# S5 mixer of the first layer: powers for the coefficient products read from a PSUM bank, their sums on GpSimd, phase squarings and one phase table on VectorE

## The chip, the cores and the metric

The kernel runs on one core of one Trainium2 chip. It is one program for a whole four-layer network on a sequence of 512 tokens. The metric is the device time of one execution in microseconds (us). Three runs of the kernel before took 1901.83, 1901.47 and 1900.82 us, median 1901.47.

## The reference, cut to what matters

The network has two blocks of two layers each, width 1024, all in float32. Only the mixer of the very first layer is touched, a state-space model (S5) with 64 groups of 16 channels and 64 complex states for each group:

```
u = (rms_norm(x) @ w_in)  as 64 groups x 16 channels
a = exp(lam * step)                        # one complex decay per group and state
b = cmul(f(a, lam), b)                     # input matrix 64 x 16 per group
x_t = a * x_(t-1) + b @ u_t                # complex recurrence over 512 tokens
y = Re(c @ x) + d * u
z = gelu(y);  out = val * sigmoid(gate),   val, gate = split(z @ w_glu)
```

The kernel works in chunks of eight tokens. For that it needs, for each group, the products of b and of c with the powers a^0 to a^8, complex, and for the recurrence over the 64 chunks it turns the complex state by a phase that grows with the chunk, then scans real numbers. The phases stand in "phase tables" (cosine and sine of 64 chunks for each group), which are made by doubling: from the phase powers e, e^2, e^4, ... each step computes the upper half of a table from its lower half.

## The kernel before, in words

The program is one list of instructions for the whole network. A class `Plan` records every operation that the code issues and works out who depends on whom from the regions of memory. One call of `emit` at the end puts all of them in a fixed order on each engine, by modelled costs and due times. So an edit in one place can move instructions elsewhere on all engines. One helper line issues all of them: L262 before, L263 after. For a PSUM bank the region is the whole bank.

In front of everything stands `layer0_mix`, which works on eight blocks m of eight groups (128 channels) each:

- `s5_params` computes the decay and the phase of each group from the inputs, on tiles of 128 partitions x 32 columns (the 8 x 64 states of a block are four columns of 128, and there are eight blocks). It squares the phase eight times to get the phase powers (tile `es`), with a normalisation after the third. One `square` is five GpSimd operations.
- `s5_table` makes one of four phase tables, for 8 of the 32 columns, in five doubling steps from width 2 to 64. Each step is two products and two sums. All four tables are made on GpSimd, tables 0 and 1 before the loop over the blocks and tables 2 and 3 within it.
- `s5_p` and `s5_q` make the coefficient matrices P = b x powers and Q = c x powers of a block. Both call `s5_cprod`: four products of 128x512 elements on VectorE, each with both operands spread by repeated reading, and two sums. The four products go to a ring of four buffers (tag `s5t`). The sums of P are on VectorE for blocks 0 and 1 and on GpSimd for blocks 2 to 7; all sums of Q are on VectorE.
- TensorE projects u block by block (`project`, 24 matmuls with split operands each), transposes P and multiplies for the kernels of a chunk (`s5_k`, `s5_pt`). `s5_u` multiplies a projection from its bank by the norm row `sbc` (a copy of a bank that all projections share). `s5_x` reads the states' input from a bank, multiplies it by cosine and sine on VectorE (the first rotation, two operations of 128x512), adds on GpSimd, scans and turns back.

Projections hold banks 0, 1, 2, 3, 5 and 6 before, in turn; 4 and 7 serve the small products. A bank of a projection comes free when `s5_u` has read it.

In the rows below, `s` is any tile of `layer0_mix`, `bank` a PSUM bank.

Of the kernel before, what the change touches and what calls it, by code (L numbers as in the profile page):

```python
# [24 lines left out]
KC = D // P  # L25
# [50 lines left out]
class Plan:  # L76
# [65 lines left out]
    @staticmethod  # L142
    def region(ap):

        if isinstance(ap, View):
            return ap.region()
        t, pat = ap.tensor, ap.ap
        if ap.space == bass.MemoryType.DRAM:
            return t.name, 0, 1, 0, 1
        if ap.space == bass.MemoryType.PSUM:  # L150
# [375 lines left out]
class Net:  # L526
# [306 lines left out]
    def s5_params(self, pool, prm):  # L833
# [13 lines left out]
        sq, c2 = mk_("sq"), mk_("c2")  # L847

        def square(yr, yi, xr, xi):
            G.tensor_tensor(sq, xi, xi, ALU.mult)  # L850
            G.tensor_tensor(c2, xr, xr, ALU.mult)
            G.tensor_tensor(yi, xr, xi, ALU.mult)
            G.tensor_tensor(yi, yi, yi, ALU.add)
            G.tensor_tensor(yr, c2, sq, ALU.subtract)
# [71 lines left out]
    def s5_table(self, pool, q, E):  # L926
# [6 lines left out]
        for i in range(1, 6):  # L933
# [21 lines left out]
    def s5_cprod(self, pool, out, x, tb, op0, op1, swap, E):


        V = self.nc.vector

        def prod(r, q):  # L960
            t = pool.tile([P, 4, 8, 16], F32, name=self.n("t"), tag="s5t", bufs=4)
            V.tensor_tensor(t, x[:, :, r].unsqueeze(2).to_broadcast([P, 4, 8, 16]),
                            tb[:, :, q].unsqueeze(3).to_broadcast([P, 4, 8, 16]), ALU.mult)
            return t.rearrange("p w j k -> p w (j k)")

        a, b = prod(0, 0), prod(1, 1)
        yield
        E.tensor_tensor(out[:, :, 0], a, b, op0)
        yield
        a, b = prod(1, 0), prod(0, 1)  # L970
        yield
        if swap:
            a, b = b, a
        E.tensor_tensor(out[:, :, 1], a, b, op1)

    def s5_q(self, pool, m, ld):

        q = pool.tile([P, 4, 2, P], F32, name=self.n("Q"), tag="s5Q", bufs=3)
        return q, self.s5_cprod(pool, q, ld[1], self.af[:, 4 * m : 4 * m + 4], ALU.add, ALU.subtract, True, self.nc.vector)

    def s5_p(self, pool, m, ld):

        pp = pool.tile([P, 4, 2, P], F32, name=self.n("P"), tag="s5P", bufs=1)
        return pp, self.s5_cprod(pool, pp, ld[0], self.pw[:, 4 * m : 4 * m + 4, :, 8:0:-1], ALU.subtract, ALU.add, False,
                                 self.nc.vector if m < 2 else self.nc.gpsimd)

    def s5_k(self, pool, m, bh, q):

# [116 lines left out]
    def layer0_mix(self, pool):  # L1105
# [9 lines left out]
            self.stat_add("n", self.x[m], m)  # L1115

        zs = []
        self.banks(g=(0, 1, 2, 3, 5, 6), r=(4, 7), s=(7,), o=(4,))
# [37 lines left out]
        sbc = self.bcast(pool, self.rms_col("n", D), 1)  # L1156
        next(params)
        next(params, None)
        self.drain(self.s5_table(pool, i, G) for i in range(2))
# [46 lines left out]
        def whole(start, gens, m):  # L1206
            start(m)
            while m in gens:
                go(gens, m)

        for m in range(6):
            project(m)
# [14 lines left out]
        for i in range(KC + 2):  # L1227
# [26 lines left out]
            go(qg, m)  # L1254
            go(qg, m)
            go(qg, m)
            if i == 0:
                project(7, lambda: w7)
                self.banks(g=(0, 1, 2, 3), r=(4, 5, 7), y=(6,))
            if 0 <= i - 2 < KC:  # L1260
                glu_part(i - 2)
            if 0 <= i - 1 < KC:
                zt[i - 1] = self.s5_o(pool, yt.pop(i - 1))
            if m < KC:
                prep_pe(m)
        self.banks(g=(4, 5, 6, 7), s=(4, 5), t=(6,), o=(7,))
        for m in range(2):
            glu(m, parts[2 * m], parts[2 * m + 1])
# [958 lines left out]
```

## Time and profile before

| | kernel before |
|---|---|
| runs | 1901.83, 1901.47, 1900.82 us; median 1901.47 |
| profiled execution | 1901.8 us, of which span of the instructions 1899.8 us |
| mean granted TensorE clock | 0.98 |
| TensorE busy | 1835.4 us, 97% of the span |
| VectorE busy | 1169.3 us, 62% |
| ScalarE busy | 837.1 us, 44% |
| GpSimd busy | 578.1 us, 30% |
| DMA | 157.85 MB, mean 83 GB/s |

The shares are means over the whole program. The touched work lies in the first 270 us, most of it between 30 and 155 us, so that the stretches there have to be read by themselves. In a window's row an engine is followed by its busy time and its number of instructions. [...]

### The profile page before, as it was taken

The numbers are of one execution on the slowest core, as the hardware profiler recorded it, in microseconds if no ns is written. First come the engines' busy times: TensorE is split into PE (matmuls) and PEld (weight loads), VectorE is DVE, ScalarE is ACT, GpSimd is POOL, SyncE is SP. The second block draws the span as 40 slices with busy tenths as digits, with TensorE's granted clock in tenths as the row PEclk, the third lists the DMA queues.
The fourth block names the chain that finished last, engine by engine and source line by source line (L and its number), as shares of the span: only waits on it lengthen the run. The fifth ranks groups of instructions, "written<-read, shape, count | busy, mean of one in ns | idle before, by whom it ended". The sixth has DMA issues, their size and how long they took to land.

```text
span 1899.8 us, 26981 instructions
## 1 busy us (share of the span) xinstructions
PE 1835.4 (97%) x10272; PEld 1474.4 (78%) x10272; DVE 1169.3 (62%) x2196; ACT 837.1 (44%) x1562; POOL 578.1 (30%) x707
## 2 busy tenths in 40 slices
PE   8789999999999999999999999999999999989997
PEld 5456788888888777778888888988778788768877
DVE  9898455444354778755534434563888763488875
ACT  4123342223233477744222222344767643566764
POOL 8984111001012166611100101540542071154205
PEclk9879999999999999999999999999999999999999
DMA  5322333323323221022232333332122132212113
GB/s 174 89 62 77 100 98 91 98 90 94 104 89 89 91 68 38 24 72 89 89 100 89 91 98 97 112 103 88 34 67 68 57 100 89 78 34 68 57 56 111
DMA packets 73136, 157.85 MB, mean 83 GB/s; under 512 B 26416, under 2 KB 34864, under 8 KB 73008
## 3 DMA queue, kind: packets, MB, share of 16 engines
q1 hardware_dynamic: 73008, 156.15, 27.0%
q8 instruction: 80, 1.31, 0.3%
q14 instruction: 48, 0.39, 0.1%
HBM read 150.81 MB, written 4.72 MB: 82 GB/s over the span
## 4 chain that ended last, share of the span: by engine, by line
PE 77%; DVE 8%; POOL 8%; ACT 4%; issue 2%; DMA 1%; SPq 0%; ACTq 0%; DVEq 0%; POOLq 0%
PE bank L262 77%; POOL s L262 3%; DVE bl L262 3%; DVE s L262 2%; POOL x L262 2%; POOL bl L262 1%; ACT bl L262 1%; DVE wl_r L262 1%; POOL acc_r L262 1%; ACT wh_r L262 1%; DVE xl_r L262 1%; DVE x L262 1%; ACT xh_r L262 0%; ACT bh L262 0%; DVE sm_r L262 0%
## 5 line engine op out<-in xcount | busy, mean ns | idle before, releaser
L262 ACT ACTIVATE wh_r<-wr_r 128x1024 fp32r<-128x1024 f32 (+2 forms) x270 | 278.1, 1031 | 587.0 <-PE bank L262 531.7
L262 PE MATMUL bank<-xh_r,wl_r 128*128 128x512 f32 (+1 forms) x1312 | 504.2, 388 | 4.5 <-DVE wl_r L262 4.4
L262 PE MATMUL bank<-xl_r,wh_r 128*128 128x512 f32 (+1 forms) x1312 | 504.6, 388 | 0.6 <-DVE xl_r L262 0.4
L262 PE MATMUL bank<-xh_r,wh_r 128*128 128x512 f32 (+1 forms) x1312 | 503.1, 389 | 1.1 <-ACT wh_r L262 1.1
L262 DVE TENSOR_TENSOR wl_r<-wr_r,wh_r 128x1024 fp32r<-128x1024 f32 (+2 forms) x270 | 372.3, 1380 | 159.2 <-ACT wh_r L262 153.1
L262 PEld LDWEIGHTS bank<-xh_r,wl_r 128*128 128x128 f32 x1312 | 249.0, 190 | 58.7 <-DVE wl_r L262 6.2
L262 PEld LDWEIGHTS bank<-xh_r,wh_r 128*128 128x128 f32 x1312 | 248.1, 190 | 55.6 <-issue 3.0
L262 PEld LDWEIGHTS bank<-xl_r,wh_r 128*128 128x128 f32 x1312 | 248.8, 190 | 52.5 <-issue 3.1
L262 POOL TENSOR_TENSOR ff<-ff,ff 128x512 f32<-128x512 f32 x44 | 62.6, 1422 | 590.2 <-DVE ff L262 575.0
L262 PE MATMUL bank<-ff,wh_r 128*128 128x512 f32 (+1 forms) x816 | 224.7, 363 | 0.3 <-ACT ff L262 0.2
L262 DVE TENSOR_TENSOR ff<-bank,ff 128x512 f32<-128x512 f32 x88 | 60.8, 691 | 223.5 <-PE bank L262 223.4
L262 PE MATMUL bank<-bh,wh_r 128*128 128x512 f32 (+1 forms) x656 | 179.3, 356 | 1.3 <-ACT bh L262 0.9
L262 PEld LDWEIGHTS bank<-ff,wh_r 128*128 128x128 f32 x816 | 145.3, 188 | 27.6 <-DVE ff L262 1.1
L262 PE MATMUL bank<-ff,wl_r 128*128 128x512 f32 (+1 forms) x408 | 146.6, 364 | 1.0 <-DVE wl_r L262 1.0
L262 DVE TENSOR_TENSOR x<-x,bank 128x256 f32<-128x256 f32 (+1 forms) x112 | 57.5, 529 | 130.9 <-PE bank L262 130.8
L262 PEld LDWEIGHTS bank<-bh,wh_r 128*128 128x128 f32 x656 | 113.9, 192 | 18.0 <-issue 2.4
L262 POOL TENSOR_TENSOR acc_r<-acc_r,sq_r 128x256 f32<-128x256 f32 (+1 forms) x63 | 75.0, 1191 | 160.8 <-ACT sq_r L262 160.7
L262 POOL TENSOR_TENSOR s<-s,s 128x32 f32<-128x32 f32 (+6 forms) x138 | 113.4, 846 | 30.4 <-DVE s L262 27.2
L262 PE MATMUL bank<-bh,wl_r 128*128 128x512 f32 (+1 forms) x328 | 113.6, 356 | 0.0
L262 DVE TENSOR_TENSOR s<-s,s 128x512 f32<-128x512 f32 (+4 forms) x124 | 93.9, 803 | 8.6 <-POOL s L262 8.3
L262 ACT ACTIVATE ff<-ff 128x512 f32<-128x512 f32 x88 | 55.0, 626 | 74.4 <-POOL ff L262 68.9
L262 PEld LDWEIGHTS bank<-ff,wl_r 128*128 128x128 f32 x408 | 76.3, 188 | 13.5 <-DVE wl_r L262 1.2
(257 smaller groups left out, 2834.2 us busy)
## 6 DMA issues: line engine op xcount, KB each, us to landing
wr_r<-w_gu SPq DMA_DIRECT2D x88, 512.0 KB, 3.5
wr_r<-w_in2f SPq DMA_DIRECT2D x48, 512.0 KB, 3.2
wr_r<-w_dn SPq DMA_DIRECT2D x37, 448.0 KB, 3.4
wr_r<-w_out SPq DMA_DIRECT2D x22, 512.0 KB, 3.3
wr_r<-w_dn SPq DMA_DIRECT2D x16, 512.0 KB, 3.5
wr_r<-w_in2v SPq DMA_DIRECT2D x16, 512.0 KB, 3.8
wr_r<-w_glu SPq DMA_DIRECT2D x12, 512.0 KB, 3.6
wr_r<-w_o SPq DMA_DIRECT2D x8, 512.0 KB, 3.2
```

The lines of the kernel that those rows point to most:

```text
L262: lambda: f(*[real(v) for v in a], **{x: real(v) for x, v in k.items()}), load, rows, idle))
```

## The change

- The eight squarings and the normalisation run on VectorE. A `square` has four operations in place of five (46 GpSimd operations of 128x32 become 38 on VectorE).
- Phase table 0 is made on VectorE; tables 1, 2 and 3 stay on GpSimd.
- A new function `s5_powers` has ScalarE copy the powers for the coefficient products into bank 7: two copies for blocks 0 to 3 at once, then two for each of blocks 4 to 7 when the place of an earlier block comes free (ten copies). `s5_cprod` reads the powers there, as its first operand.
- Both sums of P are on GpSimd for all blocks, and the second of the two sums of Q. With that 12 of the 20 sums that VectorE made are GpSimd's.
- Projections have five banks (0, 1, 2, 3, 5) in place of six, small products 4 and 6; bank 7 belongs to the powers until the end of the loop. For this bank the planner tells regions apart (`parted`).

```
 class Plan:
...
+    parted = None
...
-        if ap.space == bass.MemoryType.PSUM:
+        if ap.space == bass.MemoryType.PSUM and t.name != Plan.parted:
             return t.name, 0, P, 0, 2048
...
         sq, c2 = mk_("sq"), mk_("c2")
 
         def square(yr, yi, xr, xi):
-            G.tensor_tensor(sq, xi, xi, ALU.mult)
-            G.tensor_tensor(c2, xr, xr, ALU.mult)
-            G.tensor_tensor(yi, xr, xi, ALU.mult)
-            G.tensor_tensor(yi, yi, yi, ALU.add)
-            G.tensor_tensor(yr, c2, sq, ALU.subtract)
+            V.tensor_tensor(sq, xi, xi, ALU.mult)
+            V.tensor_tensor(c2, xr, xr, ALU.mult)
+            V.scalar_tensor_tensor(yi, xr, 2.0, xi, ALU.mult, ALU.mult)
+            V.tensor_tensor(yr, c2, sq, ALU.subtract)
 
         cr, ci = mk_("cr"), mk_("ci")
         square(cr, ci, cs, sn)
         dr, di = mk_("dr"), mk_("di")
         square(dr, di, cr, ci)
         square(cr, ci, dr, di)
-        G.tensor_tensor(sq, ci, ci, ALU.mult)
-        G.tensor_tensor(c2, cr, cr, ALU.mult)
-        G.tensor_tensor(sq, sq, c2, ALU.add)
-        G.tensor_scalar(sq, sq, -0.5, 1.5, ALU.mult, ALU.add)
+        V.tensor_tensor(sq, ci, ci, ALU.mult)
+        V.tensor_tensor(c2, cr, cr, ALU.mult)
+        V.tensor_tensor(sq, sq, c2, ALU.add)
+        V.tensor_scalar(sq, sq, -0.5, 1.5, ALU.mult, ALU.add)
 
         es = self.es = pool.tile([P, 6, w, 2], F32, name="es")
-        G.tensor_tensor(es[:, 0, :, 0], cr, sq, ALU.mult)
-        G.tensor_tensor(es[:, 0, :, 1], ci, sq, ALU.mult)
+        V.tensor_tensor(es[:, 0, :, 0], cr, sq, ALU.mult)
+        V.tensor_tensor(es[:, 0, :, 1], ci, sq, ALU.mult)
         for i in range(1, 6):
             square(es[:, i, :, 0], es[:, i, :, 1], es[:, i - 1, :, 0], es[:, i - 1, :, 1])
         yield
...
             E.tensor_tensor(tab[:, :, 1, n : 2 * n], k1[:, :, 1], k2[:, :, 0], ALU.add)
             yield
 
+    def s5_powers(self, m0, m1):
+
+        g, to = slice(4 * m0, 4 * m1), slice(m0 % 4 * 4, (m1 - 1) % 4 * 4 + 4)
+        SC = self.nc.scalar
+        SC.activation(self.powers[:, 0, to], self.pw[:, g, :, 8:0:-1], AF.Copy)
+        SC.activation(self.powers[:, 1, to], self.af[:, g], AF.Copy)
+
     def s5_load(self, pool, m):
         g4 = slice(4 * m, 4 * m + 4)
         ld = lambda nm, w: pool.tile([P, 4, 2, w], F32, name=self.n(nm), tag="s5" + nm, bufs=2)
...
 
         def prod(r, q):
             t = pool.tile([P, 4, 8, 16], F32, name=self.n("t"), tag="s5t", bufs=4)
-            V.tensor_tensor(t, x[:, :, r].unsqueeze(2).to_broadcast([P, 4, 8, 16]),
-                            tb[:, :, q].unsqueeze(3).to_broadcast([P, 4, 8, 16]), ALU.mult)
+            V.tensor_tensor(t, tb[:, :, q].unsqueeze(3).to_broadcast([P, 4, 8, 16]),
+                            x[:, :, r].unsqueeze(2).to_broadcast([P, 4, 8, 16]), ALU.mult)
             return t.rearrange("p w j k -> p w (j k)")
 
         a, b = prod(0, 0), prod(1, 1)
         yield
-        E.tensor_tensor(out[:, :, 0], a, b, op0)
+        E[0].tensor_tensor(out[:, :, 0], a, b, op0)
         yield
         a, b = prod(1, 0), prod(0, 1)
         yield
         if swap:
             a, b = b, a
-        E.tensor_tensor(out[:, :, 1], a, b, op1)
+        E[1].tensor_tensor(out[:, :, 1], a, b, op1)
 
     def s5_q(self, pool, m, ld):
 
         q = pool.tile([P, 4, 2, P], F32, name=self.n("Q"), tag="s5Q", bufs=3)
-        return q, self.s5_cprod(pool, q, ld[1], self.af[:, 4 * m : 4 * m + 4], ALU.add, ALU.subtract, True, self.nc.vector)
+        return q, self.s5_cprod(pool, q, ld[1], self.powers[:, 1, m % 4 * 4 : m % 4 * 4 + 4], ALU.add, ALU.subtract, True,
+                                (self.nc.vector, self.nc.gpsimd))
 
     def s5_p(self, pool, m, ld):
 
         pp = pool.tile([P, 4, 2, P], F32, name=self.n("P"), tag="s5P", bufs=1)
-        return pp, self.s5_cprod(pool, pp, ld[0], self.pw[:, 4 * m : 4 * m + 4, :, 8:0:-1], ALU.subtract, ALU.add, False,
-                                 self.nc.vector if m < 2 else self.nc.gpsimd)
+        return pp, self.s5_cprod(pool, pp, ld[0], self.powers[:, 0, m % 4 * 4 : m % 4 * 4 + 4], ALU.subtract, ALU.add, False,
+                                 (self.nc.gpsimd, self.nc.gpsimd))
 
     def s5_k(self, pool, m, bh, q):
...
             self.stat_add("n", self.x[m], m)
 
         zs = []
-        self.banks(g=(0, 1, 2, 3, 5, 6), r=(4, 7), s=(7,), o=(4,))
+        self.banks(g=(0, 1, 2, 3, 5), r=(4, 6), s=(6,), o=(4,))
+        self.powers = self.bank[7].rearrange("p (a w r j) -> p a w r j", a=2, w=16, r=2)
+        Plan.parted = self.powers.tensor.name
         self.warm(pool.tile([P, 2, S], F32, tag="s5PT", bufs=2)[:, 0])
         prm = pool.tile([P, 3, 32], F32, name="prm")
         nc.urgent = True
...
         sbc = self.bcast(pool, self.rms_col("n", D), 1)
         next(params)
         next(params, None)
-        self.drain(self.s5_table(pool, i, G) for i in range(2))
+        self.s5_powers(0, 4)
+        self.drain(self.s5_table(pool, i, (V, G)[i]) for i in range(2))
         us, scr, ld, pp, pg, q, qg, ks, kt, pt, zt, xg_, yt, wa = ({} for _ in range(14))
 
         def project(m, w=None):
...
             start(m)
             while m in gens:
                 go(gens, m)
+            if gens is qg:
+                self.s5_powers(m + 4, m + 5)
 
         for m in range(6):
             project(m)
...
             go(qg, m)
             go(qg, m)
             go(qg, m)
+            if m + 4 < KC:
+                self.s5_powers(m + 4, m + 5)
             if i == 0:
                 project(7, lambda: w7)
-                self.banks(g=(0, 1, 2, 3), r=(4, 5, 7), y=(6,))
+                self.banks(g=(0, 1, 2, 3), r=(4, 5), y=(6,))
             if 0 <= i - 2 < KC:
                 glu_part(i - 2)
             if 0 <= i - 1 < KC:
                 zt[i - 1] = self.s5_o(pool, yt.pop(i - 1))
             if m < KC:
                 prep_pe(m)
+        Plan.parted = None
         self.banks(g=(4, 5, 6, 7), s=(4, 5), t=(6,), o=(7,))
         for m in range(2):
             glu(m, parts[2 * m], parts[2 * m + 1])
```

GpSimd, in the place of the first sums of P that it makes. Tile s5_25 is phase table 1, s5_56 and s5_57 the temporaries of a table's step, s5_42 the phase powers, s5_64 the matrix P, s5_45, s5_46, s5_53 and s5_54 the ring of products, s5_28 a matrix Q. Before:

```order
L262 TENSOR_TENSOR s5_56_296<-s5_25_265,s5_42_282 128x256
L262 TENSOR_TENSOR s5_57_297<-s5_25_265,s5_42_282 128x256
L262 TENSOR_TENSOR s5_25_265<-s5_56_296,s5_57_297 128x8x16 x2
L262 TENSOR_TENSOR s5_56_296<-s5_25_265,s5_42_282 128x512
L262 TENSOR_TENSOR s5_57_297<-s5_25_265,s5_42_282 128x512
L262 TENSOR_TENSOR s5_64_304<-s5_45_285,s5_46_286 128x4x128
L262 TENSOR_TENSOR s5_25_265<-s5_56_296,s5_57_297 128x8x32
L262 TENSOR_TENSOR s5_64_304<-s5_53_293,s5_54_294 128x4x128
```

After (s5_26 and s5_27 are tables 2 and 3, the row of sm4 belongs to the norm):

```order
L263 TENSOR_TENSOR sm4_r1_75_115<-sm4_r0_73_114,mhalf_81 128x4
L263 COPY s5_25_265<-s5_42_282 128x16
L263 COPY s5_26_266<-s5_42_282 128x16
L263 COPY s5_27_267<-s5_42_282 128x16
L263 TENSOR_TENSOR s5_64_304<-s5_45_285,s5_46_286 128x4x128
L263 TENSOR_TENSOR s5_64_304<-s5_53_293,s5_54_294 128x4x128
L263 TENSOR_TENSOR s5_56_296<-s5_25_265,s5_42_282 128x32
L263 TENSOR_TENSOR s5_28_268<-s5_54_294,s5_53_293 128x4x128
L263 TENSOR_TENSOR s5_57_297<-s5_25_265,s5_42_282 128x32
```

Before, the sums of block 2's P stand behind the large steps of table 1; now the sums of block 0 stand ahead of table 1's first step.

VectorE, around the copy of the norm row (s5_35, `sbc`). s5_44 and s5_58 are the powers of P and a block's b, s5_47 to s5_50 temporaries of the parameters, wl_r the low part of a weight. Before, the copy is the engine's instruction 100:

```order
L262 TENSOR_TENSOR s5_46_286<-s5_58_298,s5_44_284 128x512
L262 TENSOR_TENSOR s5_48_288<-s5_48_288,s5_49_289 128x32
L262 TENSOR_TENSOR s5_49_289<-s5_15_255,s5_1_241 128x32
L262 TENSOR_TENSOR s5_64_304<-s5_45_285,s5_46_286 128x4x128
L262 TENSOR_TENSOR s5_50_290<-s5_48_288,s5_47_287 128x32
L262 TENSOR_TENSOR s5_48_288<-s5_44_284,s5_1_241 128x32
L262 COPY s5_35_275<-bank7_76 128x512
L262 TENSOR_TENSOR wl_r2_141_125<-wr_r0_5_87,wh_r2_139_124 128x1024
```

After, it is instruction 175 (s5_24 is table 0, s5_59 and s5_61 are a block's c and b, s5_32 is u, bank7 the powers):

```order
L263 TENSOR_TENSOR s5_53_293<-bank7_76,s5_59_299 128x512
L263 TENSOR_TENSOR s5_56_296<-s5_24_264,s5_42_282 128x512
L263 TENSOR_TENSOR s5_57_297<-s5_24_264,s5_42_282 128x512
L263 TENSOR_TENSOR s5_28_268<-s5_45_285,s5_46_286 128x4x128
L263 TENSOR_TENSOR s5_24_264<-s5_56_296,s5_57_297 128x8x32
L263 TENSOR_TENSOR s5_54_294<-bank7_76,s5_59_299 128x512
L263 TENSOR_TENSOR s5_24_264<-s5_56_296,s5_57_297 128x8x32
L263 COPY s5_35_275<-bank6_75 128x512
L263 TENSOR_TENSOR s5_45_285<-bank7_76,s5_61_301 128x512
L263 TENSOR_TENSOR s5_32_272<-bank0_69,s5_35_275 128x512
```

The whole of the squarings and of table 0 now stands ahead of this copy, and with it ahead of the first product of `s5_u`, which frees bank 0.

TensorE, where the first three projections with split operands end (xh_r and xl_r are the halves of the input, wh_r and wl_r of the weight). Before, the next projection goes to a sixth bank:

```order
L262 MATMUL bank5_74<-xl_r7_61_111,wh_r2_139_124 128x512
L262 MATMUL bank5_74<-xh_r7_59_110,wl_r2_141_125 128x512
L262 MATMUL bank7_76<-ident_77,s5_64_304 128x128 x4
L262 MATMUL bank6_75<-xh_r0_31_96,wh_r0_125_118 128x512
L262 MATMUL bank6_75<-xl_r0_33_97,wh_r0_125_118 128x512
L262 MATMUL bank4_73<-s5_28_268,s5_60_300 32x128 x7
```

After:

```order
L263 MATMUL bank5_74<-xl_r7_61_111,wh_r2_139_124 128x512
L263 MATMUL bank5_74<-xh_r7_59_110,wl_r2_141_125 128x512
L276 MATMUL bank4_73<-ident_77 32x128 x6
L263 MATMUL bank4_73<-s5_28_268,s5_60_300 32x128
L263 MATMUL bank6_75<-ident_77,s5_64_304 128x128 x4
L263 MATMUL bank4_73<-s5_28_268,s5_60_300 32x128 x7
L263 MATMUL bank0_69<-xh_r0_31_96,wh_r0_125_118 128x512
```

The fourth of these projections goes to bank 0 now, which the first product of `s5_u` has to have read, and the matmuls of block 0's P and Q stand ahead of it.

## Rows read from the trace of the kernel before

**Rows 1.** The page: TensorE's granted clock in 40 slices of the span, and a busy line.

```profile
PEclk9879999999999999999999999999999999999999
...
PE 1835.4 (97%) x10272; PEld 1474.4 (78%) x10272; DVE 1169.3 (62%) x2196; ACT 837.1 (44%) x1562; POOL 578.1 (30%) x707
```

**Rows 2.** The chain that ended last, in order of time: start us, us, what.

```profile
32.91 29.55 POOL s L262 x47
...
70.93 3.28 POOL s L262 x3
...
74.24 3.47 DVE s L262 x3
...
77.84 6.71 PE bank L262 x61
...
120.04 30.62 PE bank L262 x285
```

**Rows 3.** Windows: stretch, its us, each engine's busy us (count), granted clock, DMA share, GB/s.

```profile
30.00:65.70 35.70, 34.61 (x203) 26.04 (x202) 35.56 (x52) 9.17 (x13) 35.05 (x60) 0.98 0.54 147
65.70:77.84 12.14, 0.04 (x1) 0.03 (x1) 3.84 (x5) 0.00 (x0) 11.59 (x21) 0.63 0.19 52
77.84:152.40 74.56, 66.21 (x648) 42.95 (x649) 69.65 (x80) 17.80 (x33) 62.78 (x68) 0.81 0.29 73
sum 122.40, PE 100.86 PEld 69.02 DVE 109.05 ACT 26.97 POOL 109.42; mean PE 33.62 PEld 23.01 DVE 36.35 ACT 8.99 POOL 36.48
```

**Rows 4.** Windows of the stretches with the clock at 0.50, and of what follows.

```profile
68.90:82.50 13.60, 4.66 (x32) 3.35 (x34) 8.26 (x9) 1.39 (x3) 13.37 (x18) 0.50 0.15 30
103.00:109.80 6.80, 6.09 (x48) 3.83 (x44) 6.80 (x9) 0.28 (x1) 6.80 (x7) 0.50 0.15 44
120.10:137.10 17.00, 17.00 (x105) 10.52 (x106) 15.14 (x16) 2.88 (x6) 14.32 (x16) 0.50 0.31 81
152.40:268.00 115.60, 115.59 (x789) 87.59 (x790) 62.98 (x76) 40.57 (x58) 23.28 (x20) 1.00 0.29 85
```

**Rows 5.** Timeline of TensorE at 78 us: start, us, instruction, idle before.

```profile
77.84 0.45 PE L262 MATMUL bank<-ident,s 128*128 128x128 f32 x1 [12.10 <-DVE s L262]
```

**Rows 6.** Timeline of VectorE at 74 us.

```profile
74.24 2.86 DVE L262 TENSOR_TENSOR s<-s,s 128x512 f32<-128x512 f32 x2 [8.30 <-POOL s L262]
```

**Rows 7.** Groups on VectorE, 30 to 152.4 us: busy us, mean ns of one, idle before.

```profile
L262 DVE TENSOR_TENSOR s<-s,s 128x512 f32<-128x512 f32 x85 | 73.5, 912 | 8.4 <-POOL s L262 8.3
...
L262 DVE TENSOR_TENSOR s<-s,s 128x32 f32<-128x32 f32 x7 | 1.5, 215 | 0.1
```

**Rows 8.** Groups on VectorE, 0 to 350 us.

```profile
L262 DVE TENSOR_TENSOR s<-s,s 128x512 f32<-128x512 f32 x102 | 87.4, 905 | 8.5 <-POOL s L262 8.3
```

**Rows 9.** Groups on VectorE, 89.3 to 90.6 us: the two bank products of one rotation.

```profile
L262 DVE TENSOR_TENSOR s<-bank,s 128x512 f32<-128x512 f32 x2 | 1.3, 676 | 0.0
```

**Rows 10.** Groups on VectorE, 35.94 to 37.1 us: u(0) from its bank; a product.

```profile
L262 DVE TENSOR_TENSOR s<-bank,s 128x512 f32<-128x512 f32 x1 | 1.1, 1137 | 0.0
L262 DVE TENSOR_TENSOR s<-s,s 128x512 f32<-128x512 f32 x1 | 0.7, 682 | 0.0
```

**Rows 11.** Groups on GpSimd, 73.1 to 74.1 us: a sum of P.

```profile
L262 POOL TENSOR_TENSOR s<-s,s 128x512 f32<-128x512 f32 x1 | 1.3, 1264 | 0.0
```

**Rows 12.** Groups on GpSimd, 0 to 350 us: all its sums and products of this shape.

```profile
L262 POOL TENSOR_TENSOR s<-s,s 128x512 f32<-128x512 f32 x20 | 30.4, 1530 | 7.2 <-DVE s L262 5.7 <-PE bank L262 1.3
```

**Rows 13.** Groups on VectorE, 4 to 30 us: the small operations of the parameters.

```profile
L262 DVE SCALAR_TENSOR_TENSOR s<-s,s 128x32 f32<-128x32 f32 x34 | 4.6, 184 | 0.2
```

**Rows 14.** Window of the squarings and table 0 on GpSimd.

```profile
30.30:64.80 34.50, 33.41 (x200) 25.42 (x199) 34.36 (x49) 9.17 (x13) 33.99 (x58) 0.99 0.53 144
```

**Rows 15.** Timeline of TensorE at 47 us: the first matmul into the sixth bank.

```profile
47.38 0.48 PE L262 MATMUL bank<-xh_r,wh_r 128*128 128x512 f32 x1
```

**Rows 16.** Groups on ScalarE, 30 to 152.4 us: its small copies from a bank.

```profile
L262 ACT ACTIVATE s<-bank 128x128 f32<-128x128 f32 x6 | 1.7, 278 | 15.7 <-PE bank L262 15.7
```

More of the change, by code (lines that the diff above doesn't have):

```diff
@@ L85 @@
     FILL, FLOOR = 0.22, 0.95
+    parted = None
     EVERY_TABLE = (AF.Copy, AF.Identity, AF.Square)
@@ L149, in region @@
             return t.name, 0, 1, 0, 1
-        if ap.space == bass.MemoryType.PSUM:
+        if ap.space == bass.MemoryType.PSUM and t.name != Plan.parted:
             return t.name, 0, P, 0, 2048
@@ L944, in s5_table, with s5_powers @@
             yield
+    def s5_powers(self, m0, m1):
+        g, to = slice(4 * m0, 4 * m1), slice(m0 % 4 * 4, (m1 - 1) % 4 * 4 + 4)
+        SC = self.nc.scalar
+        SC.activation(self.powers[:, 0, to], self.pw[:, g, :, 8:0:-1], AF.Copy)
+        SC.activation(self.powers[:, 1, to], self.af[:, g], AF.Copy)
     def s5_load(self, pool, m):
@@ L967, in s5_cprod @@
         yield
-        E.tensor_tensor(out[:, :, 0], a, b, op0)
+        E[0].tensor_tensor(out[:, :, 0], a, b, op0)
         yield
@@ L973, in s5_cprod @@
             a, b = b, a
-        E.tensor_tensor(out[:, :, 1], a, b, op1)
+        E[1].tensor_tensor(out[:, :, 1], a, b, op1)
     def s5_q(self, pool, m, ld):
         q = pool.tile([P, 4, 2, P], F32, name=self.n("Q"), tag="s5Q", bufs=3)
-        return q, self.s5_cprod(pool, q, ld[1], self.af[:, 4 * m : 4 * m + 4], ALU.add, ALU.subtract, True, self.nc.vector)
+        return q, self.s5_cprod(pool, q, ld[1], self.powers[:, 1, m % 4 * 4 : m % 4 * 4 + 4], ALU.add, ALU.subtract, True,
+                                (self.nc.vector, self.nc.gpsimd))
     def s5_p(self, pool, m, ld):
         pp = pool.tile([P, 4, 2, P], F32, name=self.n("P"), tag="s5P", bufs=1)
-        return pp, self.s5_cprod(pool, pp, ld[0], self.pw[:, 4 * m : 4 * m + 4, :, 8:0:-1], ALU.subtract, ALU.add, False,
-                                 self.nc.vector if m < 2 else self.nc.gpsimd)
+        return pp, self.s5_cprod(pool, pp, ld[0], self.powers[:, 0, m % 4 * 4 : m % 4 * 4 + 4], ALU.subtract, ALU.add, False,
+                                 (self.nc.gpsimd, self.nc.gpsimd))
     def s5_k(self, pool, m, bh, q):
@@ L1117, in layer0_mix @@
         zs = []
-        self.banks(g=(0, 1, 2, 3, 5, 6), r=(4, 7), s=(7,), o=(4,))
+        self.banks(g=(0, 1, 2, 3, 5), r=(4, 6), s=(6,), o=(4,))
+        self.powers = self.bank[7].rearrange("p (a w r j) -> p a w r j", a=2, w=16, r=2)
+        Plan.parted = self.powers.tensor.name
         self.warm(pool.tile([P, 2, S], F32, tag="s5PT", bufs=2)[:, 0])
@@ L1158, in layer0_mix @@
         next(params, None)
-        self.drain(self.s5_table(pool, i, G) for i in range(2))
+        self.s5_powers(0, 4)
+        self.drain(self.s5_table(pool, i, (V, G)[i]) for i in range(2))
         us, scr, ld, pp, pg, q, qg, ks, kt, pt, zt, xg_, yt, wa = ({} for _ in range(14))
@@ L1209, in whole @@
                 go(gens, m)
+            if gens is qg:
+                self.s5_powers(m + 4, m + 5)
         for m in range(6):
@@ L1256, in layer0_mix @@
             go(qg, m)
+            if m + 4 < KC:
+                self.s5_powers(m + 4, m + 5)
             if i == 0:
                 project(7, lambda: w7)
-                self.banks(g=(0, 1, 2, 3), r=(4, 5, 7), y=(6,))
+                self.banks(g=(0, 1, 2, 3), r=(4, 5), y=(6,))
             if 0 <= i - 2 < KC:
@@ L1265, in layer0_mix @@
                 prep_pe(m)
+        Plan.parted = None
         self.banks(g=(4, 5, 6, 7), s=(4, 5), t=(6,), o=(7,))
```

25 lines of the change are left out of this document (12 added, 13 removed).

## The prediction

> **What bounds the kernel now.** I read the page first, then the chain of waits in order of time, then windows over the stretches that it names, and last the groups and timelines inside them. The page gives TensorE 97% of the span, but the clock line dips in the first three slices, some 140 us, and nowhere else [rows 1]. The chain says who leads there: GpSimd from 32.91 us with 47 instructions, and again at 70.93, then VectorE, and from 77.84 on mostly TensorE, without a break from 120.04 [rows 2]. The 47 are the squarings and table 0 with the head of table 1. So the stretch in question runs from 30 to 152.4 us, 122.4 us long. TensorE works 100.86 of them and idles 21.5 [rows 3]. After it TensorE is busy 115.59 of 115.60 us at full clock [rows 4] and its order there is much as before, so what is won before 152 us is carried to the end, and no more than that.
>
> The 21.5 have one large piece: 12.10 us before 77.84, where TensorE waits for VectorE [rows 5]. VectorE itself idles 8.30 of these for GpSimd before the two products at 74.24 [rows 6]: they need a buffer of the ring, which the sums of P of block 2 still have to read, and these stand behind the large steps of table 1 on GpSimd. The other waits are 1.1 us before 65.7 (35.70 less 34.61) and 8.35 after 77.84 (74.56 less 66.21) [rows 3].
>
> Beside the idle time there is the clock. [...]
>
> **The change part by part.**
>
> *Squarings and table 0 leave GpSimd.* They filled it: 33.99 of 34.50 us with 58 instructions [rows 14]. Three copies and the first steps of table 1 are part of that and stay, about 1.4 us; 32.6 us go. Then table 1 can start some 30 us earlier, and block 2's sums no longer stand behind it at the point where VectorE wants the buffer. The 12.1 us gap goes with its cause.
>
> *What VectorE takes on.* The 38 small operations cost 0.184 us as the parameters' own of that shape did [rows 13], or 0.215 as in this stretch [rows 7]: 38 x 0.2 = 7.6 us. Table 0 is two memsets, a copy and 20 products and sums, 2976 elements for each partition. From 32 elements at 0.215 [rows 7] to 512 at 0.682 [rows 10] an element adds 0.97 ns and an operation has some 0.1 us of its own, so 2.9 + 2.3 = 5.2 us. Together 12.8 us.
>
> *What VectorE gives up.* Twelve sums of 128x512 go to GpSimd. The mean of this shape in the stretch is 0.865 us by its busy time (73.5 over 85) [rows 7], so 10.4 us. The 64 products get one operand from a bank. The row before this change has no product with a step of 0 from a bank. The two nearest: the rotation's products read a bank and a tile and took 676 ns while GpSimd was at work [rows 9], and the first product of u, which reads both in steps of eight elements, took 1137 [rows 10]. Products between two tiles average 912 [rows 7], yet the same shape takes 682 at its best [rows 10]; the rest is time lost beside GpSimd. I take 676, since spread operands out of tiles already run at 682, so a step of 0 costs nothing of itself: 64 x (912 - 676) = 15.1 us. 85 of the 102 instructions of this form lie in the stretch [rows 7, 8], so of 25.5 some 21.2 us count there. VectorE's balance is 21.2 - 12.8 = 8.4 us less: 109.05 becomes 100.6 [rows 3].
>
> [...]
>
> *What GpSimd takes on.* Twelve sums at 1.264 us [rows 11] to 1.530 us, the mean of this shape [rows 12]: 15.2 to 18.4 us. Its 109.42 us of the stretch [rows 3] become 92 to 95. That is less than before, but close to the 102 that the stretch would then last, and the sums of blocks 0 and 1 are new on the way to TensorE's transposes.
>
> *The ten copies on ScalarE.* A copy of 128 elements takes 278 ns [rows 16]; two are of 256 (0.45 by the same rate as an estimate), eight of 64. That is 3 us beside an engine that is busy 26.97 of 122.4 [rows 3], at nothing. A copy for a later block waits until the last product of an earlier block has read its place; behind it on ScalarE stand copies out of banks and conversions of weights for which TensorE waits. I count that within the range.
>
> *Five banks in place of six.* The new work of VectorE stands ahead of the norm row's copy and of u(0), which frees bank 0. u(0) started at 35.9 [rows 10]. With 12.8 us ahead of it, it starts at 48.7; six more products go ahead of it too, which would make 52.8 if nothing fell behind in exchange. Before, projections 2 to 4 kept TensorE busy until 47.38, where the sixth bank came in [rows 15]. So it may wait 2 to 6 us there. If the cover is gone altogether, the price is the 12.8.
>
> **The sum.** Idle time: six sums of P and Q of blocks 0 and 1 now stand on GpSimd between VectorE's products and TensorE; with no lead at all they cost 6 x 1.264 = 7.6 us [rows 11], and the wait for u(0) falls into the same time. I take 8 us as what stays of 21.5, a gain of 13.5. Bounds: nothing stays (21.5), or 9.4 of the old waits and the 7.6 stay, 17 in all (4.5). Clock: the low stretch at the gap goes, 4.66 busy; of the 17.00 I let half go, and the 6.09 stays, since VectorE is nearly full all the time and TensorE will still have short waits. Low busy time falls by 13.2, worth 6.6 us. Bounds: 0 and 13.9. Together 13.5 + 6.6 = 20.1 us.
>
> Check against VectorE: the stretch would last 102.3 us and VectorE work 100.6 of it. That is tight, but 52.6 of the 115.6 us after it are free on VectorE [rows 4], so some work can slip there. If none slips and the 5.0 us of its other waits (122.4 - 109.05 - 8.3) [rows 3, 7] stay, the stretch takes 105.6: a gain of 16.8.
>
> The profiled execution took 1901.8 us, so 1881.7; the median lies 0.3 us lower, which makes the forecast 1881.4. Its own range is 1877 to 1885.
>
> **Rivals.**
>
> *GpSimd takes the place of the gap, or the clock stays low.* GpSimd makes twelve more sums, each at twice the time that VectorE needs alone (1264 against 682 [rows 10, 11]), and holds both buffers of the ring until then. If that keeps the waits short but many, the clock doesn't rise: only the first low stretch goes (2.3 us), and idle falls by the 12.1 less two sums that are waited for in full (2.5), and by the 1.1 before 65.7: 2.3 + 9.6 + 1.1 = 13 us, 1888.5. For it: VectorE's wait at 74 was for just such a sum [rows 6]. Against it: the large steps ahead of that sum move away. [...]
>
> *u(0) late.* If bank 0 comes free only after all of the 12.8 us, and TensorE has nothing else, then 7.3 of the 20.1 are left: 1894.1. Against it: matmuls of block 0's P and Q can go before.
>
> *The bank reads are slow, so that the product isn't cheaper.* The price is that of u's product, 1137 ns [rows 10]. VectorE: 109.05 - 8.7 (the sums in the stretch) + 53.3 products x 0.225 = 12.0 + 12.8 = 125.1; with its 5.0 us of waits 130.1, against 122.4 now. That is 7.7 slower, 1909.5. It decides from 0.99 us for one product, where VectorE fills the old stretch. For it: steps in both operands, as u's product has. Against it: at 912 in the mean and 682 at best, steps of 0 from tiles cost nothing. In this case the change doesn't do what moving the operand promises.
>
> *More goes.* All idle time and all low clock: 21.5 + 13.9 = 35.4 us, 1866; with half of what the forecast leaves, some 28 us, 1874. VectorE's balance speaks against it, unless much of its work slips behind 152 us.
>
> **How the numbers follow.** Forecast 0.53, GpSimd or clock 0.18, u(0) late 0.07, more goes 0.10, slow bank reads 0.08, and 0.04 that it all cancels within 0.2%, about 3.8 us, which is what a measurement of this kernel can tell. Faster is the sum of the first four, 0.88. The range goes from 1871 to 1895: it leaves out the slow reads, the cancelling and the far part of "more goes", somewhat under 2 in 10.
>
> **What would show it.** The 12 us gap of TensorE near 66 to 78 is gone, and GpSimd has no row of 128x32 squarings. VectorE shows 64 products of 128x512 from a bank near 0.68 us; near 0.9 the contention isn't lifted, near 1.1 the slow rival holds. Its small operations stand at 0.2 us. The first rotation (65.3 us now) and the work at 152 come earlier by some 20 us, and the clock between 100 and 130 is mostly 1.00. A gap of TensorE at 47 us of more than 6 us would mean that u(0) is late; TensorE waiting for GpSimd sums would mean the first rival. The forecast is wrong if TensorE's idle time from 30 us to the end of this stretch stays above 15 us.

## The result and the profile after

Four runs of the changed kernel took 1879.64 to 1883.2 us, median 1880.72. The ratio to the kernel before is 0.9894, with a 95% interval of 0.988 to 0.9908. The forecast was 1881.4. The time was right; the reasons were only half right, as the experiments show.

The profiled execution took 1880.23 us, its span 1878.5. First the page's clock line, to be read beside [rows 1]:

```profile
PEclk8999999999999999999999999999999999999999
```

One slice is below 9 where there were two; the first slice itself went from 9 to 8. Now windows of the kernel after: the stretch that does the work of 30 to 152.4 us before (TensorE's 849 matmuls against 851), what follows it up to the load of the next layer's weights, and the two places after 30 us where the clock stood at 0.50:

```profile
30.00:131.60 101.60, 90.58 (x849) 63.17 (x850) 99.34 (x172) 30.50 (x58) 80.05 (x101) 0.96 0.43 110
131.60:249.93 118.33, 117.53 (x796) 88.17 (x795) 62.06 (x73) 39.77 (x57) 26.93 (x26) 1.00 0.29 85
30.00:35.00 5.00, 4.19 (x12) 3.51 (x13) 4.93 (x18) 2.12 (x2) 2.63 (x4) 0.50 0.37 113
55.50:58.90 3.40, 3.19 (x11) 2.47 (x12) 3.21 (x7) 0.86 (x2) 3.24 (x7) 0.50 0.65 197
```

Against [rows 3] the stretch is 122.40 - 101.60 = 20.8 us shorter. TensorE idles 101.60 - 90.58 = 11.0 us in it, where it idled 21.5: 10.5 us gained. It is busy 90.58 against 100.86, 10.3 us less for the same matmuls. That is the clock: 7.4 us of its work stand at half speed now, 27.75 before [rows 4]. The prediction counted three stretches at half speed there; a fourth, which begins earlier, reaches 1.30 us into the stretch, with TensorE busy throughout. So it was 29.05 us before, and half of the difference, an estimate from the 0.50 and 1.00 of the clock, is 10.8. That fourth stretch has become longer; first before, then after:

```profile
24.50:31.30 6.80, 5.74 (x18) 4.79 (x19) 6.77 (x16) 0.36 (x1) 6.06 (x11) 0.50 0.44 143
```

```profile
24.70:35.00 10.30, 6.26 (x16) 4.67 (x17) 10.23 (x35) 2.51 (x3) 4.82 (x4) 0.50 0.36 112
```

GpSimd is busy 80.05 in place of 109.42, VectorE 99.34 in place of 109.05. After the stretch some of it is given back: the load of the next layer's weights comes 18.9 us earlier, by the two chains of waits, first before, then after:

```profile
268.90 4.20 DMA mh<-w_kr
```

```profile
249.98 3.92 DMA mh<-w_kr
```

The remaining 2.4 of the span's 21.3 us come later in the program and were not followed up.

What TensorE waits for in 30 to 152.4 us after (engine and tile waited for: us, times, longest):

```profile
PE bank L263 <- POOL s L263: 4.2, 6, 1.5
PE bank L263 <- DVE wl_r L263: 3.0, 2, 2.2
PE bank L263 <- ACT s L263: 2.9, 5, 0.9
PE bank L263 <- POOL sm_r L263: 1.7, 1, 1.7
PE bank L263 <- DVE s L263: 0.9, 3, 0.4
```

No wait is longer than 2.2 us; the one of 12.10 [rows 5] is gone. VectorE's groups of 0 to 350 us after, and five operations on a bank in a row at 110 us, a rotation's and four coefficient products:

```profile
L263 DVE TENSOR_TENSOR s<-bank,s 128x512 f32<-128x512 f32 x88 | 59.2, 716 | 2.6 <-ACT bank L263 2.0 <-PE bank L263 0.3 <-POOL s L263 0.2
...
L263 DVE TENSOR_TENSOR s<-s,s 128x512 f32<-128x512 f32 x28 | 21.4, 802 | 0.1
...
L263 DVE TENSOR_TENSOR s<-bank,s 128x512 f32<-128x512 f32 x5 | 3.1, 674 | 0.0
```

The 88 are 64 products, 16 of the rotation and the eight slow ones of u. A product from the bank takes 674 ns, where the mean from tiles was 912 [rows 7]. GpSimd shows the other side. Its groups of 0 to 350 us, first before, then after:

```profile
L262 POOL TENSOR_TENSOR s<-s,s 128x256 f32<-128x256 f32 x32 | 29.0, 920 | 7.9 <-DVE s L262 7.7
L262 POOL TENSOR_TENSOR s<-s 128x32 f32<-128x32 f32 x31 | 18.1, 603 | 3.2 <-DVE s L262 3.1
L262 POOL TENSOR_TENSOR s<-s,s 128x252 f32<-128x252 f32 x16 | 16.6, 1045 | 13.9 <-DVE s L262 13.9
```

```profile
L263 POOL TENSOR_TENSOR s<-s,s 128x512 f32<-128x512 f32 x30 | 42.1, 1407 | 8.8 <-DVE s L263 8.5
L263 POOL TENSOR_TENSOR s<-s,s 128x256 f32<-128x256 f32 x28 | 24.8, 895 | 7.4 <-DVE s L263 7.0
...
L263 POOL TENSOR_TENSOR s<-s,s 128x252 f32<-128x252 f32 x16 | 12.1, 763 | 11.4 <-DVE s L263 11.4
```

The squarings (x31) are gone, but operations that the change doesn't touch are faster too: those of 128x252 took 1045 ns and take 763. The mean of 128x512 went from 1530 [rows 12] to 1407, in a group that now holds twelve sums more and two products of table 0 less. The prediction had no term for this.

### The profile page after: what moved, and what is told of

Read it like the earlier page. It is cut to its first block, busy times and chain, and to the rows that moved or that the text cites. A ratio compares the mean times of both kernels' runs of the same rounds, so it can differ in the third digit from the quotient of the medians.

```text
span 1878.5 us, 26997 instructions
## 1 busy us (share of the span) xinstructions
PE 1822.5 (97%) x10270; PEld 1464.9 (78%) x10270; DVE 1158.0 (62%) x2245; ACT 838.9 (45%) x1572; POOL 546.5 (29%) x650
## 4 chain that ended last, share of the span: by engine, by line
PE 75%; DVE 8%; POOL 5%; ACT 4%; issue 2%; DMA 1%; SPq 0%; ACTq 0%; DVEq 0%; POOLq 0%
PE bank L263 75%; DVE bl L263 3%; DVE s L263 2%; POOL x L263 2%; POOL bl L263 1%; ACT bl L263 1%; POOL acc_r L263 1%; DVE wl_r L263 1%; ACT wh_r L263 1%; DVE x L263 1%; ACT xh_r L263 0%; ACT bh L263 0%; DVE sm_r L263 0%; DVE xl_r L263 0%; ACT xl_r L263 0%
## 5 line engine op out<-in xcount | busy, mean ns | idle before, releaser
L263 POOL TENSOR_TENSOR s<-s,s 128x256 f32<-128x256 f32 (+6 forms) x116 | 96.3, 858 | 34.9 <-DVE s L263 33.3
L263 ACT ACTIVATE bl<-bank 128x256 f32<-128x256 f32 (+3 forms) x142 | 62.9, 453 | 52.9 <-PE bank L263 51.7
```

Source lines behind the costliest of these rows:

```text
L263: lambda: f(*[real(v) for v in a], **{x: real(v) for x, v in k.items()}), load, rows, idle))
```

## The experiments

Two theories stood against each other. The prediction's: the gap of 12 us is made by squarings and tables in GpSimd's queue and goes when they leave it. The rival: VectorE and GpSimd slow each other as long as VectorE reads two tiles, and the bank reads alone carry the gain. Three parts can be on or off; all eight kernels were run, each in turns with the kernel before on the same chip (medians 1901.0 to 1901.6):

| kernel | bank reads | phases on VectorE | sums on GpSimd | median us | ratio to before, 95% interval |
|---|---|---|---|---|---|
| before | - | - | - | 1901.6 | 1 |
| e5 | - | yes | - | 1906.69 | 1.0028 (1.0013 to 1.0044) |
| e6 | - | - | yes | 1914.43 | 1.0065 (1.0051 to 1.0079) |
| e1 | - | yes | yes | 1907.17 | 1.0035 (1.0023 to 1.0047) |
| e4 | yes | - | - | 1876.06 | 0.9868 (0.9854 to 0.9882) |
| e2 | yes | - | yes | 1877.16 | 0.9874 (0.986 to 0.9887) |
| e3 | yes | yes | - | 1887.51 | 0.993 (0.9917 to 0.9942) |
| after | yes | yes | yes | 1880.72 | 0.9894 (0.988 to 0.9908) |

"Phases" are squarings, normalisation and table 0. The program plans the order of all engines anew in e2 to e6 and e12, so their differences hold the new place of the work and the new order together. In e1 and e7 to e11 an order is kept, and only these compare one thing alone.

**e1: only the operand's place differs.** The order of all engines is that of the changed kernel.

```
-  self.powers[:, 0, m % 4 * 4 : m % 4 * 4 + 4]
+  self.pw[:, 4 * m : 4 * m + 4, :, 8:0:-1]      # and self.af for Q
```

> The changed kernel with its order on every engine kept, instruction for instruction; only the operand of the 64 coefficient products differs: they read the powers from their tiles in SBUF, as before the change, and no longer from bank 7 (ScalarE still makes the ten copies). If the operand's place is what counts (two operands from tiles collide with GpSimd): the products take 0.85 to 0.95 us in the mean against about 0.68, 64 x 0.2 = 13 us more on VectorE, which is nearly full, GpSimd's sums grow too, and the time rises to 1893 to 1902 us. If the new order and division of work is what counts (theory of the prediction for the gap: squarings and table 0 leave GpSimd's queue): the gap of 12 us stays away and only a part of the 13 us shows, 1883 to 1890 us. If neither place nor contention matters: 1881.

Measured: 1907.17 us, over the whole range and slower than before the change. The groups of 0 to 350 us of e1 on VectorE and GpSimd:

```profile
L263 DVE TENSOR_TENSOR s<-s,s 128x512 f32<-128x512 f32 x92 | 81.9, 936 | 1.3 <-POOL s L263 1.2
...
L263 DVE TENSOR_TENSOR s<-bank,s 128x512 f32<-128x512 f32 x24 | 19.0, 813 | 1.3 <-PE bank L263 1.3
```

```profile
L263 POOL TENSOR_TENSOR s<-s,s 128x512 f32<-128x512 f32 x30 | 49.9, 1668 | 9.4 <-DVE s L263 8.5 <-PE bank L263 0.7
...
L263 POOL TENSOR_TENSOR s<-s,s 128x252 f32<-128x252 f32 x16 | 16.3, 1024 | 14.1 <-DVE s L263 14.1
```

With the same 30 operations, 24 sums and 6 products of the tables, GpSimd takes 1668 ns for one where it takes 1407 beside bank reads. VectorE's 116 operations of this shape take 81.9 + 19.0 = 100.9 us; the same 116 take 59.2 + 21.4 = 80.6 in the changed kernel. As the order is the same, the 64 products can be matched one by one in the two traces: they take 1000 ns in the mean in e1 and 678 in the changed kernel. Both engines lose. The operand's place is worth 26 us here, more than the whole change.

**e2, e3: one part taken back from the changed kernel.**

```
e2  -  V.tensor_tensor(sq, xi, xi, ALU.mult)  ...  (V, G)[i]
    +  G.tensor_tensor(sq, xi, xi, ALU.mult)  ...  G
e3  -  (self.nc.vector, self.nc.gpsimd)       # Q; P likewise as before
    +  (self.nc.vector, self.nc.vector)
```

> The changed kernel with squarings, normalisation and table 0 back on GpSimd, as before; powers from the bank and sums on GpSimd stay. Theory of the prediction (GpSimd's queue of squarings and tables makes the 12 us gap): the sums of P, now more of them, stand behind that queue again, the gap comes back at least in part, 1890 to 1905 us. Rival (bank reads alone make VectorE and GpSimd fast enough that the queue no longer matters): VectorE is rid of 12.8 us, 1876 to 1884 us.

> The changed kernel with the twelve sums back on VectorE. VectorE takes 12 x 0.68 to 0.87 = 8 to 10 us more, GpSimd 15 to 18 us less. If VectorE is the engine that TensorE waits for: 1885 to 1891 us. If GpSimd's sums are what TensorE waits for (4.2 us of its waits in the profile after the change name GpSimd): 1877 to 1881 us.

Measured: e2 1877.16, e3 1887.51 us. With the phases back on GpSimd the kernel is not slower. By the medians it is 3.6 us faster, but the two intervals overlap. The prediction's theory wanted 1890 to 1905 us, and it falls here. The sums are worth 6.8 us, as long as VectorE carries the phases.

**e4: the bank reads alone.** The kernel before with `s5_powers`, the five banks and the products from bank 7.

```
+  self.powers = self.bank[7].rearrange(...)   # s5_powers, banks and cprod's operand as in the change
   self.nc.vector if m < 2 else self.nc.gpsimd  # P; Q on nc.vector; square and tables on G
```

> The kernel before with one part of the change alone: powers copied to bank 7 and read there, with the five banks that this leaves. Squarings, tables and sums stay where they were. Theory of the prediction: VectorE saves up to 15 us, but the gap of 12 us hangs on GpSimd's queue and stays, so that only the waits of VectorE elsewhere shrink: 1892 to 1898 us. Rival (the bank reads carry the whole gain): 1878 to 1885 us.

Measured: 1876.06 us, 1.9 us below the rival's range and 16 below that of the prediction's theory. It is also 4.7 us below the changed kernel, though the two intervals just touch; e4 and e2 are the best of all. GpSimd has its squarings, and the first sum of block 2's P still stands behind the large steps of table 1. Groups on GpSimd, 0 to 350 us, and the start of that sum in its timeline:

```profile
L263 POOL TENSOR_TENSOR s<-s,s 128x512 f32<-128x512 f32 x20 | 27.5, 1384 | 2.9 <-DVE s L263 2.8
...
L263 POOL TENSOR_TENSOR s<-s,s 128x32 f32<-128x32 f32 x30 | 11.2, 385 | 0.7
L263 POOL TENSOR_TENSOR s<-s 128x32 f32<-128x32 f32 x31 | 10.7, 363 | 2.6 <-DVE s L263 2.5
...
63.35 1.29 POOL L263 TENSOR_TENSOR s<-s,s 128x512 f32<-128x512 f32 x1
```

An operation of the squarings takes 363 ns in place of 603, so the queue reaches that sum at 63.35 us; before, it began at 72.9 (70.93 + 3.28 [rows 2] less its 1.26 [rows 11]). The gap goes although nothing was taken out of the queue.

**e5, e6: each of the other parts alone**, in the kernel before, with the edits of e2 and e3 the other way.

```
e5  -  G.tensor_tensor(sq, xi, xi, ALU.mult)  ...  G
    +  V.tensor_tensor(sq, xi, xi, ALU.mult)  ...  (V, G)[i]
e6  -  self.nc.vector                         # both sums of Q; both of P go to G for all blocks
    +  (self.nc.vector, self.nc.gpsimd)
```

> The kernel before with one part alone: squarings, normalisation and table 0 on VectorE. Theory of the prediction (GpSimd's queue makes the gap): the 12 us gap goes, VectorE takes 12.8 us more, 1888 to 1896 us. Rival (collisions of VectorE's and GpSimd's reads of tiles set the pace, and products from tiles still collide): VectorE's 12.8 us show, 1900 to 1910 us.

> The kernel before with one part alone: twelve sums from VectorE to GpSimd, powers read from tiles. Theory of the prediction: VectorE wins 10.4 us, but the sums of blocks 0 and 1 now stand behind squarings and tables on GpSimd: 1898 to 1912 us. Rival (VectorE alone is the bound, the sums' place doesn't matter): 1890 to 1896 us.

Measured: 1906.69 and 1914.43 us, both slower. TensorE's waits in e5, 29 to 185 us:

```profile
PE bank L262 <- POOL s L262: 8.4, 8, 3.2
PE bank L262 <- DVE s L262: 4.5, 4, 2.1
PE bank L262 <- ACT s L262: 4.0, 2, 3.6
PE bank L262 <- POOL sm_r L262: 0.7, 1, 0.7
```

No wait is over 3.6 us: the gap did go with the queue, as the prediction had it, and it paid nothing. The waits add up to 17.6 us in small pieces all the same; VectorE has the phases on top, and its operations of 128x512 between tiles still take 875 ns in the mean. The profiled run took 1902.18 us, near the low end of the ten (1900.11 to 1914.0), so the trace shows that the gain is absent, not where the 5 us went. e6 ended over both theories' ranges.

**e7, e8: dose.** e4 with its order kept; in e7 all 64 products read tiles again, in e8 the 32 of P.

```
e8  -  self.powers[:, 0, m % 4 * 4 : m % 4 * 4 + 4]
    +  self.pw[:, 4 * m : 4 * m + 4, :, 8:0:-1]
e7  also
    -  self.powers[:, 1, m % 4 * 4 : m % 4 * 4 + 4]
    +  self.af[:, 4 * m : 4 * m + 4]
```

> The kernel of e4 (bank reads alone) with its order kept but for a few rows, five banks and ten copies, and the 64 products reading the powers from tiles again. If the operand's place is the whole of e4's gain: 1898 to 1904 us, with the gap of TensorE back and GpSimd's 128x32 operations at 0.55 us and more again. If the order that the planner found for e4, or the copies' other effects, had a share: in between, 1882 to 1895 us.

> The kernel of e4 with its order kept: the 32 products of Q read from the bank, the 32 of P from tiles again. If each product that collides costs its share: half of e4's gain of 25 us, 1885 to 1892 us. If what counts is GpSimd's queue up to block 2's sum, which a few collisions already delay past VectorE's wait: near 1900. If the chain has slack: near 1877.

Measured: e7 1901.93 us, ratio 1.0005 (0.9996 to 1.0013); e8 1889.73, 0.9934 (0.992 to 0.9947). TensorE's gap in each:

```profile
76.20 0.45 PE L263 MATMUL bank<-ident,s 128*128 128x128 f32 x1 [9.04 <-DVE s L263]
```

```profile
72.00 0.45 PE L263 MATMUL bank<-ident,s 128*128 128x128 f32 x1 [6.93 <-DVE s L263]
```

GpSimd's groups of 0 to 350 us in e7, to be read beside those of e4, whose order it has:

```profile
L263 POOL TENSOR_TENSOR s<-s,s 128x512 f32<-128x512 f32 x20 | 28.0, 1409 | 4.1 <-DVE s L263 4.0
L263 POOL TENSOR_TENSOR s<-s,s 128x32 f32<-128x32 f32 x30 | 16.6, 564 | 0.7
L263 POOL TENSOR_TENSOR s<-s,s 128x252 f32<-128x252 f32 x16 | 16.1, 1020 | 15.4 <-DVE s L263 15.4
L263 POOL TENSOR_TENSOR s<-s 128x32 f32<-128x32 f32 x31 | 15.8, 527 | 2.5 <-DVE s L263 2.5
```

e7 takes the time of the kernel before, and a gap of 9 us is back: five banks, the copies and the order of e4 together cost and bring nothing, and the operand's place is worth all of e4's gain. The squarings' operations take 527 ns here and 363 in e4. Half of the bank reads bring 12 of e4's 25 us.

**e9, e10: which engine's time.** e4 with its order kept; in e9 36 operations of the squarings are issued twice, in e10 a small copy follows each product.

```
e9   +  G.tensor_tensor(sq, xi, xi, ALU.mult)             # the same once more
e10  +  V.tensor_copy(pad, tb[...].to_broadcast([P, 4, 8, 4]))
```

> The kernel of e4 (bank reads alone), its order kept, with 36 of the 46 GpSimd operations of the squarings issued twice (the same result): about 36 x 0.36 = 13 us that GpSimd works more ahead of table 0, which puts the first sum of block 2 back from 63 us to about 75, where it was before the change (72.9). If e4's gain comes from GpSimd's queue being through earlier: the gap of TensorE is back and most of the gain lost, 1888 to 1898 us. If it comes from VectorE's shorter products: 1875 to 1880 us.

> The kernel of e4, its order kept, with a copy of 128 elements from the bank behind each of the 64 products on VectorE: 64 x 0.23 = about 15 us more on VectorE, what its products lost by reading the bank, while GpSimd keeps its relief. If e4's gain is VectorE's time: 1888 to 1893 us. If it is GpSimd's queue: 1875 to 1880 us. If both share it, this and e9 each lose about half: 1882 to 1888 us.

Measured: e9 1887.74 us (ratio 0.9927, 0.9911 to 0.9943), 0.3 under the range for GpSimd's queue; e10 1882.96 (0.9903, 0.9887 to 0.992), in the range of a shared gain. TensorE's longest wait and GpSimd's small operations in e9, and the copies in e10:

```profile
78.14 0.45 PE L263 MATMUL bank<-ident,s 128*128 128x128 f32 x1 [9.72 <-DVE s L263]
```

```profile
L263 POOL TENSOR_TENSOR s<-s 128x32 f32<-128x32 f32 x54 | 20.3, 386 | 3.9 <-DVE s L263 2.1
L263 POOL TENSOR_TENSOR s<-s,s 128x32 f32<-128x32 f32 x43 | 16.8, 399 | 1.7
```

```profile
L974 DVE COPY s<-bank 128x128 f32<-128x128 f32 x64 | 17.7, 277 | 0.0
```

GpSimd's 15.2 us more (20.3 + 16.8 against 10.7 + 11.2 in e4) bring the gap back and cost 11.7 us. VectorE's 17.7 us (277 ns for a copy, 0.23 us by the author's estimate), spread over the products, bring no gap and cost 6.9. So GpSimd's relief at that one place weighs more than VectorE's. Both pads are larger than what they stand for: these small operations lose 10.5 us in e7 (16.6 + 15.8 against 21.9), and 64 products lose 15.2 at 912 against 674 ns. Together they return 18.6 of e4's 25.5 us; the two pads in one kernel were not tried, so the other 7 stay unassigned.

**e11: the clock.** The kernel before with 48 matmuls ahead of the transposes at which TensorE waits.

```
+  for _ in range(48): matmul(bank5[:, :128], ident, ident)
```

> The kernel before, with 48 dummy matmuls of 128x128 into a free bank (48 x 0.21 = 10 us at full clock) ahead of the transposes at which TensorE waits 12.1 us; nothing else is changed. TensorE is busy in the gap, so that its clock should be granted in full behind it. If TensorE's clock is a price of its own: the 4.66 us behind the gap take half, 1899 us, and if the later two stretches at half clock go with it, 1888 to 1892 us. If TensorE only follows VectorE there: 1900.5 to 1903 us.

Measured: 1909.72 us (ratio 1.0045, 1.003 to 1.006), over both theories' ranges. TensorE's timeline (two records for each dummy), and a window at the dummies' start:

```profile
78.57 13.34 PE L1124 MATMUL bank<-ident 128*128 128x128 f32 x96 [12.99 <-DVE s L262]
```

```profile
78.50:83.60 5.10, 5.03 (x24) 5.03 (x25) 5.10 (x8) 0.00 (x0) 4.94 (x8) 0.51 0.34 69
```

The dummies themselves waited for VectorE and ran behind the gap, where they delayed the rest; the clock stood at 0.51 over their first 5.1 us, 0.42 us for a dummy. The 36 behind them took 0.23 us each, where 0.21 was the author's estimate. That a TensorE busy in the gap has its clock granted in full behind it was the author's inference from a low stretch that begins within the gap [rows 4, 5]. The run doesn't show it, as nothing ran in the gap, and before the change the clock stood at 0.50 also where TensorE was busy for 17.00 of 17.00 us [rows 4]. What the clock alone is worth stays open. The run shows one thing: 13 us more for TensorE right behind the gap cost 8.7, so it is on the path there.

**e12: table 0 alone back on GpSimd**, in the changed kernel.

```
-  self.drain(self.s5_table(pool, i, (V, G)[i]) for i in range(2))
+  self.drain(self.s5_table(pool, i, G) for i in range(2))
```

> The changed kernel with table 0 back on GpSimd; squarings stay on VectorE. VectorE has about 5 us less, GpSimd 12 to 15 more. If VectorE's time is what the moved phases cost (e2, with both back, took 1877.2): 1878 to 1880 us. If the squarings ahead of the norm row's copy are what costs: 1880 to 1882. If GpSimd is short of time with the twelve sums: over 1882.

Measured: 1879.12 us (ratio 0.9886, 0.9868 to 0.9905), between e2 and the changed kernel. The steps of 1.6 and 2.0 us are within the spread of the runs, so the 3.6 us can't be divided between table and squarings.

## Why the prediction was right, and where it was not

- **Bank reads on VectorE: right.** 676 ns were taken, 674 measured in a row at 110 us and 678 in the mean of the 64. VectorE's balance was 100.6 of 102.3 us, measured 99.34 of 101.60. The rival of slow reads is refuted by the same row. A product took 674 ns with a bank as source, and 682 without one [rows 10].
- **GpSimd's relief: the step that failed.** The prediction let GpSimd's time fall to 92 to 95 us, by the operations that came and went, each at its old price. It fell to 80.05, in the main because its own operations got faster. At the busy time for one that their shapes had in the stretch before, the 101 operations there would come to some 93 us by their groups; they come to 84.6. The other part is that five of its 30 operations of 128x512 lie outside the stretch now, where it was two of 20. The prediction had the sign in hand, products at 682 ns at best and 912 in the mean, and read it for VectorE alone; in e1 both engines lost (100.9 against 80.6 us on VectorE, 1668 against 1407 ns on GpSimd). The 682 were not VectorE without a neighbour, as one rival had it: that product ran from 37.00 us on, and GpSimd was at work on operations of 128x32 from 36.83 to 37.79.
- **"The gap goes with its cause": right in the trace of e5, wrong as a gain.** The squarings' leaving removes the gap and costs 5 us of time without bank reads (e5). With them it costs 11.4 us while VectorE has the sums (e3 against e4); beside the sums on GpSimd the 3.6 us are within overlapping intervals. In e4 the gap goes while they stay. The gap had two causes, the length of the queue and the pace at which it was worked off, and the second was the cheap one to remove.
- **Idle time and clock: the sum was right, the terms were not.** 13.5 us of idle time were forecast, 10.5 came; 6.6 us by the clock, 10.3 came. More short waits stayed than the 8 us allowed, 11.0, among them two for the weights' low parts that the prediction didn't look at (3.0 us). The clock fell only once in spite of them, at 55.5 us; that short waits keep it low, as the sum and the first rival had it, was the author's estimate and no run here shows it. The forecast took 6.6 us for 13.2 us of work at a clock of 0.50, and 13.9 for all 27.75 [rows 4]. That such work takes half the time at 1.00 was an estimate, and no run shows that term by itself. In the kernel before, the groups of 128x512 matmuls take 634 to 794 ns in the mean at 0.50 (120.1 to 137.1 us) and 398 to 400 at 1.00 (152.4 to 268 us). The two errors nearly cancel, and that is luck. So is the rest: of the 20.8 us won in the stretch 1.9 are given back behind it, where the prediction let nothing change, and 2.4 come from later in the program.
- **VectorE's load: right by two errors.** By the prediction's own rows an operation's own time is 0.215 - 32 x 0.00097 = 0.18 us and not 0.1 [rows 7, 10]. Table 0 is then 7.1 us in place of 5.2, and VectorE's balance 102.5 us, more than the 102.3 of the stretch. The shapes of table 0 add 6 to 7 us to VectorE's groups there. But 14 of the 38 small operations ran before 30 us, outside the stretch that the balance is about.
- **Sums: right in sign.** Their 10.4 us on VectorE became 6.8 beside the phases and nothing without them (e4 against e2); without bank reads the sums alone cost 12.8 (e6). TensorE waits 4.2 us for GpSimd's tiles, 7.6 were allowed.
- **Five banks and copies: right.** e7 puts them at nothing. The copies of 256 elements took 381 ns each, 0.45 us by the estimate, and the eight of 64 took 226, 2.6 us in all. The fourth split projection began at 52.62 us, where 48.7 to 52.8 was expected for u(0):

```profile
52.62 0.50 PE L263 MATMUL bank<-xh_r,wh_r 128*128 128x512 f32 x1 [0.38 <-ACT s L263]
```

In the order bank reads, phases, sums the change is worth -25.5, +11.4 and -6.8 us, together -20.9. The forecast reached that number by giving the phases a gain that the bank reads made, so the time was hit by luck as far as the phases go.

## What to carry to other kernels

Where VectorE and GpSimd work side by side, look for operations of one shape that take two different times. The difference may be a collision for which both engines pay, as here with the products (1000 against 678 ns) and GpSimd's operations of 128x512 (1668 against 1407), e1 against the changed kernel. It needn't be: u's product took 1137 ns and the rotation's 676, and both read a bank and one tile [rows 9, 10]. Keep the order and move one operand, as e7 does, to tell. Moving one operand to a bank helped here more (25.5 us, e4) than moving work between the engines, which without it cost 5 us (e5) and 13 (e6). And a long wait of the bounding engine is not a gain by itself: ask which engine is full right behind it.

## What was not expected of the hardware

That GpSimd's small operations lost most for their length here. With one order on all engines (e7 and e4), an operation of 32 elements in the squarings took 527 ns beside products from tiles and 363 beside products from the bank; one of 512 elements took 1409 and 1384. The loss isn't the same everywhere: in e1 against the changed kernel those of 512 lost too, 1668 against 1407. The chain of many small operations was the one that stood ahead of the sum for which VectorE, and so TensorE, waited.
